# An encoder layer in split float32 matmuls: tiles that begin at multiples of 256 bytes

## The chip, the cores and the metric

The kernel runs on one core of a Trainium2 chip. The metric is the device time of one execution in microseconds (us); lower is better. TensorE is called PE below, VectorE DVE, ScalarE ACT and GpSimd POOL.

## What is computed

One layer of a bidirectional encoder over 512 tokens of width 1024, in float32:

```python
x = x + 0.5 * swiglu(rmsnorm(x), w1, w3, w2)          # first FFN, width 2816
h = rmsnorm(x)
proj = h @ w_in                                       # attention A: q,k,v; attention B: q,k,v; gates
o_a = three groups of dilated window attention, 8 heads of 64, weighted by their softmax sums
o_b = grouped attention, 8 heads of 128, 2 key/value heads, per-head norm and rotary
x = x + (sigmoid(g_a) * (o_a @ P_a) + sigmoid(g_b) * (o_b @ P_b)) @ w_out
x = x + 0.5 * swiglu(rmsnorm(x), w1, w3, w2)          # second FFN
out = rmsnorm(x)
```

## The kernel before, in words

**Split matmuls.** A float32 operand is kept as two tiles of type float32r, a high part (names in H) and the rest (names in L), and one product is three matmuls into the same bank: H by H, H by L and L by H (`mm3`, lines 232 to 234). In each, one 128x128 block is the stationary operand, loaded first, and the other operand streams through with 256 or 512 columns, the moving operand. Nearly all PE time is such matmuls.

- 512 columns, 3000 matmuls: the plain projections (moving hH, hL: 768), the token projections (`token`, moving the weights wh, wl, stationary hH, hL: 576, of which 192 take every fourth column of hH as stationary), the products with w2 (`blocks`, moving gg: 984), the branch and output products (moving oH, qH, mH: 480) and those of attention B (moving kH, kL, vH, vL: 192).
- 256 columns, 4176 matmuls: the first products of both FFNs and ten blocks of the q, k projection are done by a seven-product scheme (`strassen`) on halves of the tokens. One step is 24 matmuls (two column blocks, four row blocks, three parts), its moving operand either a half of hH, hL or a tile of sums TH, TL (in the q, k projection TQ). There are 63 steps in the first FFN, 35 in the q, k projection and 70 in the second FFN, 4032 matmuls; the last 144 are the halves of the last product with w2 (moving gg).

**The order of the work.** PE's order is that of the code. The weights come by DMA into rings (wr, wa, wt), are split by ACT and DVE into the ring of wh, wl tiles, and PE takes them from there. Every fourth of these pairs, in the stages that have the room, lies in a second ring.

**Where tiles lie.** Within a partition, tiles are laid one behind the other, each rounded up to 32 bytes. One stack grows from the low end (constants, small tiles, rings, working tiles), one from the high end (hH, hL, below them rel_bias and TH, TL). So the start of a large tile follows from the small tiles that were laid before it. By the addresses in the built program, these are the starts of the tiles that split matmuls read, in bytes past a multiple of 256:

```
tiles                                    before   after
hH, hL                                      224       0
TH, TL, first FFN                           128       0
TH, TL, second FFN                          224       0
TQ                                           32       0
gg, kH, kL, vH, vL, PTH, PTL                 32       0
oH, oL, qH, qL, mH, mL                       32       0
wh, wl, first ring                          160       0
wh, wl, second ring                          32       0
```

The 32 of gg, for example, comes from the constants (they end at 160 past a multiple) and the 16-byte tiles ms, ss and rs, four of each with 32 bytes to each (384 together). hH is at 224 since the usable memory ends 32 bytes below a multiple of 256. The identity that the transposes read begins at 64, before and after.

Of the kernel before, what the change touches and what calls it, by code (L numbers as in the profile page):

```python
# [11 lines left out]
F32 = mybir.dt.float32  # L12
# [19 lines left out]
LAG = 1  # L32
LAST = 2
WARM = 4
T = 512
D = 1024
NK = 8
# [16 lines left out]
def tile_at(li):  # L54
    if li < 4:
        return 256 * li, (256 if li < 3 else 128), (0 if li < 3 else 64)
    return GP + 256 * (li - 4), 256, 256
# [8 lines left out]
def f32(t):  # L66
    return t.bitcast(F32)


class Layer:  # L70
    def __init__(self, ctx, tc, a):
        self.tc, self.nc, self.a = tc, tc.nc, a
        ctx.enter_context(tc.manual_schedule(engines={mybir.EngineType.PE}))
        pool = lambda n, **k: ctx.enter_context(tc.tile_pool(name=n, **k))
        self.dram = pool("dram", bufs=1, space=DRAM)
        self.cst = pool("cst", bufs=1)
        self.wb = pool("wb", bufs=1)
        self.tmp = pool("tmp", bufs=4)
        self.psm = pool("psm", bufs=4, space=PSUM)
        self.psa = pool("psa", bufs=4, space=PSUM)  # L80
        nc = self.nc
        c = self.cst
        self.x = [c.tile([128, T], F32, name=f"x{d}") for d in range(NK)]
        self.par = c.tile([128, 48], F32, name="par")
        nc.scalar.dma_start(self.par, a["par"])
        self.ident = c.tile([128, 128], F32, name="ident")
        self.ones = c.tile([128, 1], F32, name="ones")
        nc.vector.memset(self.ones, 1.0)
        self.mhalf = c.tile([128, 4], F32, name="mhalf")
        nc.vector.memset(self.mhalf, -0.5)  # L90
        nc.scalar.activation(self.ones, self.ones, AF.Copy)
        self.r = c.tile([128, 8], F32, name="r")
        self.R = c.tile([128, T], F32, name="R")
        nc.gpsimd.memset(self.R, 0.0)
        self.acc = c.tile([128, T], F32, name="acc")
        self.open_h()
        self.gate_d = self.dram.tile([16, 128, T], F32, name="gate_d")
        self.qk_d = self.dram.tile([2 * NSQ, 128, T], F32, name="qk_d")
        self.items = ([("v", 0), ("v", 1), ("sw", 0), ("v", 2)] + [("g", j) for j in range(2)]
                      + [("qk", f) for f in range(NSQ, 12)] + [("g", j) for j in range(2, 9)]  # L100
                      + [("b", g) for g in range(3)] + [("g", j) for j in range(9, 16)])
        span = {"v": ("wav", 4), "qk": ("waq", 2), "g": ("wg", 1), "b": ("wb", 4)}
        self.order = self.ffn_order("a")
        for kind, n in self.items:
            if kind == "sw":
                self.order += [("swq", at) for at in self.slots(range(0, NSQ, 2))]
                continue
            name, m = span[kind]
            self.order += [(name, m * n + i) for i in range(m)]
        self.order += [("wab", i) for i in range(12)] + [("wo", i) for i in range(8)]  # L110
        self.order += self.ffn_order("b")
        self.raws, self.tiles, self.used, self.wx, self.TQ = {}, [], 0, None, None
        self.cap = len(self.order)
        self.rings = {k: [] for k in BUFS}
        self.index = {it[:2]: n for n, it in enumerate(self.order)}
        self.kind = [self.home(it) for it in self.order]
        self.todo = sorted((n for n, t in enumerate(self.kind) if t != "ws"), key=self.turn_of)
# [22 lines left out]
    def open_h(self):  # L140
        self.hctx = ExitStack()
        hp = self.hctx.enter_context(self.tc.tile_pool(name="hp", bufs=1, side="right", reuse_waits="tile"))
        self.hH = [hp.tile([128, T], F32R, name=f"hH{d}") for d in range(NK)]
        self.hL = [hp.tile([128, T], F32R, name=f"hL{d}") for d in range(NK)]
# [236 lines left out]
    def rpow(self, dst, src, inv):  # L381
        nc = self.nc
        n = dst.shape[-1]
        ms = self.tmp.tile([128, 4], F32, tag="ms", name="ms")[:, :n]
        nc.vector.tensor_scalar(ms, src, inv, EPS, op0=ALU.mult, op1=ALU.add)
        nc.gpsimd.tensor_tensor(dst, ms, self.mhalf[:, :n], op=ALU.pow)

# [194 lines left out]

    def bias_open(self, bp):
        self.bp = bp
        self.rel = bp.tile([32, 24], F32, name="rel_bias")
        self.nc.sync.dma_start(self.rel, self.a["rel_bias"])
        self.zd = self.dram.tile([8, 128, NV], F32, name="zd")
        self.vd = self.dram.tile([8, NV], F32, name="vd")
# [163 lines left out]
    def scores_a(self, hp, res):  # L752
        nc, ap, qk = self.nc, self.ap, self.qk[hp]
# [11 lines left out]
        for pair in range(4):  # L765
            banks = [self.aux("S") for _ in range(2)]
            heads = []
            for h in range(2):
                hs, ps, mv = slice(64 * h, 64 * h + 64), banks[h], []
                for u in range(2):  # L770
                    li = 2 * pair + u
                    n, o = tile_at(li)[1], 256 * u
# [6 lines left out]
                    else:  # L779
                        c = slice(128 * (li - 4), 128 * (li - 4) + 128)  # L780
# [5 lines left out]
            for h in range(2):  # L786
                for u in range(2):
                    li = 2 * pair + u
                    off, n, w0 = tile_at(li)
# [4 lines left out]
            for h in range(2):  # L794
                for li in (2 * pair, 2 * pair + 1):
                    off, n, _ = tile_at(li)
# [24 lines left out]
        nc.vector.tensor_mul(L, E, SO[:, :, :, 2:4])  # L821
        nc.vector.tensor_add(MN, L[:, 0], L[:, 1])
        nc.vector.reciprocal(MN, MN)
        F = ap.tile([128, 8, 2], F32, tag="F", name="F", bufs=2)
        nc.vector.tensor_mul(F, E[:, 0], MN)
        res += [P, F]

    def values_a(self, hp, P, F):
        nc, ap, V = self.nc, self.ap, self.V
# [8 lines left out]
        def scale(stage):  # L838
            for h in range(2):
                for li in (2 * stage, 2 * stage + 1):  # L840
                    off, n, _ = tile_at(li)
                    sl = P[h][:, off:off + n]
                    nc.vector.tensor_scalar(sl, sl, F[:, li, h:h + 1], None, op0=ALU.mult)

# [109 lines left out]
    def attn_b(self, pp):  # L954
        nc = self.nc
        qH, qL, kH, kL, vH, vL = self.qH, self.qL, self.kH, self.kL, self.vH, self.vL
        P, po, pend = {}, {}, []

        def score(h, i):
            ps = self.aux("Sb")  # L960
            s = slice(128 * i, 128 * i + 128)
            self.mm3(ps, qH[:, h, s], qL[:, h, s], kH[:, h // 4, :], kL[:, h // 4, :], True, True)
            nm = pp.tile([128, 1], F32, tag="nm", name="nm", bufs=4)
            nc.vector.tensor_reduce(nm, ps, axis=mybir.AxisListType.X, op=ALU.max, negate=True)
            p = pp.tile([128, T], F32, tag="P", name="Pb", bufs=8 + LAG)
            lq = pp.tile([128, 1], F32, tag="lq", name="lq", bufs=4)
            nc.scalar.activation(p, ps, AF.Exp, bias=nm, scale=1.0, accum_out=lq)
            nc.vector.reciprocal(lq, lq)
            nc.vector.tensor_scalar(p, p, lq, None, op0=ALU.mult)
            P[h, i] = p  # L970

        def flip(h, k):
            pt = self.aux("Tb")
            for j in range(4):
                nc.tensor.transpose(pt[:, 128 * j:128 * j + 128], P[h, j][:, 128 * k:128 * k + 128], self.ident)  # L975
            H, L = self.split(pp, pt, [128, T], "PTH", "PTL")
            fs = slice(128 * (h // 4), 128 * (h // 4) + 128)
            pend.append((h, k, vH[:, k, fs], vL[:, k, fs], H, L, k == 0, k == 3))

        def value():  # L980
            h, k, *args = pend.pop(0)
            if k == 0:
                po[h] = self.bank()
            self.mm3(po[h], *args)
            if k == 3:
                nc.scalar.copy(qH[:, h, :], po[h])
                nc.vector.tensor_sub(qL[:, h, :], po[h], f32(qH)[:, h, :])

        for s in range(37 + LAG):
            if s < 32:  # L990
                score(s // 4, s % 4)
            t = s - 4 - LAG
            if 0 <= t < 32:
                flip(t // 4, t % 4)
            if pend and t > 0:
                value()
            yield GAP_B
        assert not pend
# [95 lines left out]
    def layer(self, out):  # L1094
# [4 lines left out]
        warm = self.aux("warm")  # L1099
        for _ in range(WARM):  # L1100
            nc.tensor.matmul(warm[:, :256], self.R[:, :128], self.R[:, :256], start=True, stop=True)
# [123 lines left out]
```

## Time and profile before

| | |
|---|---|
| median of three runs | 1282.46 us (1282.14 to 1282.67) |
| profiled execution, own time | 1282.78 us |
| its span, first to last instruction | 1281.0 us |
| granted clock of PE over the span | 0.998 of full speed |
| PE busy | 1266.8 us, 99% of the span |
| DVE, ACT, POOL busy | 887.8, 586.5, 118.9 us |

A matmul counts as busy from its start to its modelled end, and matmuls overlap, so the 99% says that PE always had one in flight, not that it was at its peak. What a matmul costs is read from the distance between the starts of two that follow each other, or from the length of a stretch and the number of matmuls in it.

### The profile page before, as it was taken

What the parts mean: (1) busy time and instruction counts of PE and PEld (TensorE: products, weight loads), DVE (VectorE), ACT (ScalarE), POOL (GpSimd) and SP (SyncE); (2) the same over time, 40 slices, a digit from 0 to 9 for tenths busy, and PEclk for the clock granted to TensorE, in tenths of its full rate; (3) what the DMA queues carried; (4) which work ended last, traced back from release to release, by engine and by line L of the source; (5) the groups of instructions that cost most, each with busy time, mean ns of one, the idle gap of its engine ahead of it and who ended that gap; (6) DMA issues with size and microseconds to landing.
All of it is one profiled execution on the core that took longest, in us unless ns stands there. A gap on an engine that the chain in (4) does not pass through costs nothing.

```text
span 1281.0 us, 19956 instructions
## 1 busy us (share of the span) xinstructions
PE 1266.8 (99%) x8002; PEld 1122.1 (88%) x8002; DVE 887.8 (69%) x1339; ACT 586.5 (46%) x867; POOL 118.9 (9%) x124
## 2 busy tenths in 40 slices
PE   9999999999999999999999999999999999999997
PEld 7897999899889999877888878888889989988996
DVE  7784688467783885667557898655577747874775
ACT  8551355145463442635334465543465415532553
POOL 1111101000210212100001100000301000100001
PEclk9999999999999999999999999999999999999999
DMA  8865766241484846632232210345737636743222
GB/s 298 227 187 167 182 190 189 89 109 55 144 218 142 218 131 208 189 116 85 92 111 83 99 66 25 108 163 165 237 89 181 191 90 176 196 148 104 62 83 67
DMA packets 85549, 181.91 MB, mean 142 GB/s; under 512 B 12480, under 2 KB 19024, under 8 KB 85456
## 3 DMA queue, kind: packets, MB, share of 16 engines
q1 hardware_dynamic: 67904, 140.74, 32.6%
q0 software_dynamic: 16832, 39.34, 15.2%
q8 instruction: 63, 1.03, 0.3%
q10 hardware_dynamic: 720, 0.55, 0.1%
q14 instruction: 30, 0.25, 0.1%
HBM read 168.98 MB, written 15.29 MB: 144 GB/s over the span
## 4 chain that ended last, share of the span: by engine, by line
PE 93%; DVE 3%; issue 1%; DMA 1%; ACT 1%; POOL 0%; SPq 0%; POOLq 0%; DVEq 0%
PE mm L232 24%; PE mm L234 24%; PE mm L233 24%; PE Y L232 3%; PE Y L234 3%; PE Y L233 3%; PE X L232 2%; PE X L234 2%; PE X L233 2%; PE S L785 1%; PE mm L836 1%; PE Tb L975 1%; PE T L854 1%; PE Sb L233 0%; PE Sb L234 0%
## 5 line engine op out<-in xcount | busy, mean ns | idle before, releaser
L217 ACT CAST wh<-wr 128x1024 fp32r<-128x1024 f32 x142 | 148.8, 1049 | 224.8 <-PE mm L233 142.0
L218 DVE TENSOR_TENSOR wl<-wr,wh 128x1024 fp32r<-128x1024 f32 x142 | 173.3, 1221 | 56.9 <-ACT wh L217 56.2
L232 PE MATMUL mm<-hH,wh 128*128 128x256 f32 (+1 forms) x600 | 200.5, 334 | 0.4 <-ACT hH L368 0.3
L234 PE MATMUL mm<-hH,wl 128*128 128x256 f32 (+1 forms) x600 | 196.3, 327 | 1.0 <-DVE wl L218 1.0
L233 PE MATMUL mm<-hL,wh 128*128 128x256 f32 (+1 forms) x600 | 196.1, 327 | 0.3 <-DVE hL L369 0.3
L232 PE MATMUL mm<-gg,wh 128*128 128x512 f32 (+1 forms) x376 | 143.1, 380 | 0.0
L234 PE MATMUL mm<-gg,wl 128*128 128x512 f32 (+1 forms) x376 | 142.6, 379 | 0.0
L233 PE MATMUL mm<-gg,wh 128*128 128x512 f32 (+1 forms) x376 | 142.5, 379 | 0.0
L232 PEld LDWEIGHTS mm<-hH,wh 128*128 128x128 f32 x600 | 112.9, 188 | 14.8 <-issue 3.2
L234 PEld LDWEIGHTS mm<-hH,wl 128*128 128x128 f32 x600 | 112.7, 188 | 12.4 <-DVE wl L218 1.4
L233 PEld LDWEIGHTS mm<-hL,wh 128*128 128x128 f32 x600 | 112.8, 188 | 10.1 <-DVE hL L369 0.8
L217 ACT CAST wh<-wa 128x1024 fp32r<-128x1024 f32 x48 | 50.4, 1050 | 102.5 <-PE mm L233 49.6
L500 DVE TENSOR_TENSOR u<-mm,R 128x512 f32<-128x512 f32 (+1 forms) x52 | 33.8, 649 | 85.0 <-PE mm L234 84.7
L218 DVE TENSOR_TENSOR wl<-wt,wh 128x1024 fp32r<-128x1024 f32 x48 | 58.7, 1223 | 38.1 <-ACT wh L217 37.6
L234 PE MATMUL mm<-TH,wl 128*128 128x256 f32 x304 | 84.7, 279 | 0.0
L232 PE MATMUL mm<-TH,wh 128*128 128x256 f32 x304 | 84.6, 278 | 0.0
L233 PE MATMUL mm<-TL,wh 128*128 128x256 f32 x304 | 84.6, 278 | 0.0
L232 PEld LDWEIGHTS mm<-gg,wh 128*128 128x128 f32 x376 | 70.8, 188 | 15.3 <-PE mm L234 0.9
L234 PEld LDWEIGHTS mm<-gg,wl 128*128 128x128 f32 x376 | 70.8, 188 | 14.1
L233 PEld LDWEIGHTS mm<-gg,wh 128*128 128x128 f32 x376 | 70.9, 188 | 13.8
L217 ACT CAST wh<-ws 128x1024 fp32r<-128x1024 f32 x48 | 50.4, 1051 | 71.0 <-PE mm L233 52.3
L218 DVE TENSOR_TENSOR wl<-wa,wh 128x1024 fp32r<-128x1024 f32 x48 | 58.6, 1221 | 31.2 <-ACT wh L217 31.0
(233 smaller groups left out, 3171.3 us busy)
## 6 DMA issues: line engine op xcount, KB each, us to landing
wr<-in_w2a SPq DMA_DIRECT2D x22, 512.0 KB, 3.3
wr<-in_w2b SPq DMA_DIRECT2D x22, 512.0 KB, 3.5
wt<-in_w13b SPq DMA_DIRECT2D x20, 512.0 KB, 4.1
wa<-in_w13b SPq DMA_DIRECT2D x20, 512.0 KB, 3.5
wt<-in_w13b POOLq DMA_DIRECT2D x20, 512.0 KB, 6.1
wt<-in_w13a SPq DMA_DIRECT2D x18, 512.0 KB, 3.5
wt<-in_w13a POOLq DMA_DIRECT2D x18, 512.0 KB, 6.2
wa<-in_w13a SPq DMA_DIRECT2D x18, 512.0 KB, 3.4
```

The lines of the kernel that those rows point to most:

```text
L217: self.nc.scalar.copy(H, raw)
L218: self.nc.vector.tensor_sub(L, raw, f32(H))
L232: mm(out, lH, rH, start=start, stop=False, skip_group_check=more)
L233: mm(out, lH, rL, start=False, stop=False, skip_group_check=more)
L234: mm(out, lL, rH, start=False, stop=stop, skip_group_check=more)
L500: nc.vector.tensor_mul(u, ps, R)
L785: nc.tensor.matmul(*args, start=True, stop=True)
L836: nc.tensor.matmul(oc, v, p, start=st, stop=sp)
L854: nc.tensor.transpose(ps[:, 128 * b:128 * b + 128], P[h][:, c0 + 128 * b:c0 + 128 * b + 128], self.ident)
L975: nc.tensor.transpose(pt[:, 128 * j:128 * j + 128], P[h, j][:, 128 * k:128 * k + 128], self.ident)
```

## The change

Two filler tiles, and small tiles of round sizes. `edge`, 224 bytes, is the first tile of the stack at the high end; `even`, 96 bytes, stands among the constants; nothing reads or writes either. ms, nm and lq are made 64 bytes, rel_bias 256 and F 128, of which slices of the former sizes are used. In the built program every tile that a split matmul reads begins at a multiple of 256 bytes (the table above). The built program of the change has the same instructions on every engine, in the same order, with the same waits: what differs is addresses, and the row lengths of the five enlarged tiles.

```diff
+EDGE = 224
...
+        self.edge = ctx.enter_context(tc.tile_pool(name="edge", bufs=1, side="right")).tile([128, EDGE // 4], F32, name="edge")
...
         self.r = c.tile([128, 8], F32, name="r")
+        c.tile([128, 24], F32, name="even")
...
-        ms = self.tmp.tile([128, 4], F32, tag="ms", name="ms")[:, :n]
+        ms = self.tmp.tile([128, 16], F32, tag="ms", name="ms")[:, :n]
...
-        self.rel = bp.tile([32, 24], F32, name="rel_bias")
+        self.rel = bp.tile([32, 64], F32, name="rel_bias")[:, :24]
...
-        F = ap.tile([128, 8, 2], F32, tag="F", name="F", bufs=2)
+        F = ap.tile([128, 16, 2], F32, tag="F", name="F", bufs=2)[:, :8]
...
-            nm = pp.tile([128, 1], F32, tag="nm", name="nm", bufs=4)
+            nm = pp.tile([128, 16], F32, tag="nm", name="nm", bufs=4)[:, :1]
...
-            lq = pp.tile([128, 1], F32, tag="lq", name="lq", bufs=4)
+            lq = pp.tile([128, 16], F32, tag="lq", name="lq", bufs=4)[:, :1]
```

## Rows read from the trace of the kernel before

**Rows 1.** The page: the chain that ended last, shares of the span.

```profile
PE 93%; DVE 3%; issue 1%; DMA 1%; ACT 1%; POOL 0%; SPq 0%; POOLq 0%; DVEq 0%
```

**Rows 2.** PE's longest waits: us in total, times, longest.

```profile
PE mm L836 <- DVE PT L856: 1.6, 1, 1.6
PE warm L1101 <- POOL R L94: 1.3, 1, 1.3
PE rb L401 <- POOL r L386: 1.0, 1, 1.0
```

**Rows 3.** Windows, 256-column stages: length, PE busy (matmuls), clock, DMA share, GB/s.

```profile
53.44:92.46 39.02, 39.02 (x336) 1.00 0.68 176
139.36:218.00 78.64, 78.64 (x672) 1.00 0.72 188
262.54:321.56 59.02, 59.02 (x504) 1.00 0.29 84
402.09:501.35 99.26, 99.26 (x840) 1.00 0.60 176
954.99:1012.74 57.75, 57.75 (x504) 1.00 0.71 185
1057.28:1133.53 76.25, 76.25 (x672) 1.00 0.72 189
1178.07:1235.28 57.21, 57.21 (x504) 1.00 0.29 86
1252.04:1261.90 9.86, 9.86 (x84) 1.00 0.00 0
```

**Rows 4.** Windows, 256 columns: one or two steps of 24 matmuls, start to start.

```profile
142.19:145.06 2.87, 2.87 (x26) 1.00 0.56 191
181.83:187.51 5.68, 5.68 (x50) 1.00 0.51 164
407.77:410.62 2.85, 2.85 (x26) 1.00 0.72 210
1257.74:1260.60 2.86, 2.86 (x26) 1.00 0.00 0
```

**Rows 5.** Windows, 512 columns; up to three matmuls counted only overlap an edge.

```profile
29.31:53.20 23.89, 23.89 (x107) 1.00 0.97 288
817.90:936.90 119.00, 119.00 (x515) 1.00 0.59 183
649.28:675.60 26.32, 26.32 (x115) 1.00 0.28 91
378.50:401.60 23.10, 23.10 (x98) 1.00 0.40 113
1144.80:1150.24 5.44, 5.44 (x25) 1.00 0.26 90
```

**Rows 6.** Timeline of four transposes: start, us to the last end; and the next start.

```profile
780.49 0.60 PE L975 MATMUL Tb<-ident,Pb 128*128 128x128 f32 x4
780.85 0.48 PE L232 MATMUL mm<-PTH,vH 128*128 128x512 f32 x1
```

**Rows 7.** Groups by shape: busy us, mean ns of one.

```profile
L975 PE MATMUL Tb<-ident,Pb 128*128 128x128 f32 x128 | 19.4, 273 | 0.2 <-DVE Pb L969 0.2
```

**Rows 8.** Windows, all engines, second FFN: busy of PE, weight loads, DVE, ACT, POOL.

```profile
1057.28:1133.53 76.25, 76.25 (x672) 76.25 (x671) 62.23 (x62) 41.53 (x47) 8.43 (x7) 1.00 0.72 189
```

## The prediction

> **What bounds the kernel now.** I read the chain of waits first: 93% of the span is PE, and DVE, DMA and ACT share the rest [rows 1]. Then PE's waits: the longest is 1.6 us and there are a handful [rows 2]. So PE is not waiting for tiles; the time is the number of matmuls times their pace. The pace is therefore what I looked at next, in stretches that hold split matmuls of one width alone.
>
> For 256 columns the stages do not agree, although their matmuls have the same shape [rows 3]. In the first FFN 336, 672 and 504 matmuls take 39.02, 78.64 and 59.02 us: 116.1, 117.0 and 117.1 ns each. The q, k projection takes 118.2 (99.26 us over 840). The second FFN, which issues the same steps as the first, takes 114.6, 113.5 and 113.5. The last half products take 9.86 us over 84, 117.4, or about 119 when the two that only overlap an edge are taken off. The granted clock is 1.00 in every one of these rows, which is the 2.4 GHz level. It is not traffic either: the slow last row has a DMA share of 0.00, and in the second FFN 0.72 and 0.29 give the same 113.5 [rows 3]. What differs between the stages is where their tiles begin. In the second FFN all moving tiles begin at 224 past a multiple of 256; in the first, TH is at 128 and hH at 224; in the projection TQ is at 32 and hH at 224.
>
> Single steps say the same [rows 4]. A step with TH at 128 takes 119.6 ns a matmul (2.87 us over 24) when its weights lie in the second ring, at 32, and 118.3 (5.68 us over 48) when they lie in the first, at 160. TQ at 32 with weights at 32 takes 118.8 (2.85 over 24), and gg at 32 with weights at 32 takes 119.2 (2.86 over 24).
>
> For 512 columns [rows 5], with the edge matmuls taken off: hH at 224 with weights at 160 takes 229.7 (23.89 us over 104); tiles at 32 with weights at 160 take 232.4 (119.00 over 512); the token products 233 (26.32 over 113), and where the stationary operand takes every fourth column 238 (23.10 over 97). Moving gg at 32 with weights also at 32 takes 226.7 (5.44 over 24).
>
> **What the change does, part by part.** No instruction is added, removed or moved, and no wait changes. The fillers are never touched, and the larger small tiles are used in the same sizes, so those edits cost nothing in themselves. DVE's and ACT's instructions on tiles at new starts could take another time, but in the densest stage DVE is busy 62.23 of 76.25 us and ACT 41.53 [rows 8], so a few per cent there stay covered; were DVE 20% slower it would reach PE's 76 us. Loads land at new starts too; DMA is 1% of the chain, most of it at the start [rows 1]. I take zero for these, within 2 us either way. What is left is the pace of 7176 split matmuls. No row shows a tile at 0 past a multiple of 256, so each width is bounded by the nearest rows.
>
> *512 columns.* After the change moving and stationary tiles begin at the same place, as gg and the second ring do now, at 32 both. That row is the nearest: 227 ns. By classes: 1200 matmuls at 32 with weights at 160, (232.4 - 227) ns each, 6.5 us; 768 with hH at 224, (229.7 - 227), 2.1 us; 384 token products in contiguous columns, (233 - 227), 2.3 us; together 10.9 us. The 192 with every fourth column I leave, since what sets them apart stays (2.1 us if they go to 227 too). Bounds: nothing gained, or 10.9 + 2.1 = 13.0 us; below 227 see the third rival.
>
> *256 columns.* The stages of rows 3 that make up the 4032 add up to 467.15 us, 115.9 ns each. The lower bound is the second FFN's best, 113.5: 457.6 us, 9.5 us less, and 0.8 us less in the last 144 (119 to 113.5). The upper bound is what the same rows say of moving and stationary at the same place, 119.2: 480.6 us, 13.5 us more. The two neighbours point to opposite ends. I choose by what the second FFN has and the others lack: its moving tiles all begin at one place, while weights alternate between 160 and 32 without harm, and it has the fastest of all stages. After the change there is one place for everything. I take the mean of that FFN, (57.75 + 76.25 + 57.21) us over 1680, 113.8 ns: 458.9 us, 8.3 us less, and 0.7 for the last 144, 9.0 us in all.
>
> The sum is 10.9 + 9.0 = 20 us. The profiled execution took 1282.78 us with a span of 1281.0, and the median of the runs is 1282.46, 0.3 us from it; from the median the forecast is 1262 us.
>
> **A rule weighed.** Two 512-column matmuls with gg at 32 stand 227 or 232 ns apart, by whether their weights begin at 32 or at 160 [rows 5], so the read of the weights does reach into the moving stream. The Trainium skill, SBUF — State Buffer, SBUF: two separate sides, says that PE never waits on anyone at its memory ports; by it the pace would have nothing to do with where tiles lie, and the time would stay at 1282.5. The rows do not agree with it for two reads of PE itself.
>
> **Rivals.**
>
> *Tiles that begin at the same place get in each other's way (slower).* For it: the two 256-column rows with both at 32 are among the slowest (118.8 and 119.2), and TH at 128, the only moving tile that begins at a multiple of 128, is slow too (118.3 and 119.6) [rows 4]: being rounder is no help there. With 256 columns a weight load must fit into the time of one matmul; with 512 it has twice that, so a collision could cost the one and not the other. Against it: rows with one and the same collision should be slow at 512 too, and are the fastest. Price: 13.5 us lost at 256 columns, 10.9 won at 512, 1285 us; if the 512 columns do not gain, 1296. It decides from a mean of 115.9 + 10.9 us / 4032 = 118.6 ns on.
>
> *Nothing changes.* All tiles begin at a multiple of 32 now, and if the unit that matters is no larger, the differences between stages come from something else that the change leaves, such as distances between tiles. 1282.5 us, give or take 3. The Trainium skill, SBUF — State Buffer, Specifications (TRN2), gives lines of 16 bytes, and by that unit alone no line would be saved; no run here shows the unit.
>
> *The floor falls.* The fastest rows, 113.5 and 227, are in one ratio to the columns, 0.443 ns each, and all their moving tiles begin off a multiple of 64. Four transposes take 0.60 us with a last one of 273 ns, so they start (600 - 273) / 3 = 109 ns apart [rows 6, 7]. If a start at a round place lets 256 columns pass in 109 and 512 in 218, the sum is 4032 x 6.9 + 144 x 10 = 29 us and 1200 x 14.4 + 768 x 11.7 + 384 x 15 + 456 x 9 = 36 us, 65 us, 1217 us; half of it is 1250. Against it: TH at 128 does begin at a multiple of 64 and shows none of this. The Trainium skill, TensorE: Matmul & The Clock Gate, Back-to-back issue gap, gives columns / 2.4 + 2.5 ns, 109 and 216; by it the time would be an estimate of 1211.
>
> **How the numbers follow.** Forecast, a gain of 10 to 30 us: 0.38. Floor falls, a gain beyond that: 0.14. Nothing, or gains and losses that cancel within some 10 us: 0.22. Collisions, a loss of more than that or of nearly that: 0.26. About 0.2%, 2.6 us, is what a measurement of this kernel can tell from no change. Of the cancelling cases a little under half lies within it, and the rest falls on both sides: faster 0.56, same 0.11, slower 0.33. The range for 8 in 10 leaves out the deep half of the fallen floor and the worst collisions (no gain at 512 columns and 119.6 at 256): 1228 to 1297. The likeliest case alone spans 1252 to 1273.
>
> **What would show it.** In the profile after, the stretches of rows 3 and 5 hold the same matmuls, so their lengths compare one to one. Right: the first FFN's and the projection's steps as quick as the second FFN's, near 113.5 to 114, and the products with w2 and the branches near 227. The floor has fallen if any 512-column stretch is below 224. The collision rival shows as 119 and more in the second FFN, which is at 113.5 now. Wrong in its base would be a PE that begins to wait, for instance on DVE's wl tiles, or a pace that still differs between stages although all tiles begin alike.

## The result, and the profile after

The change makes the kernel slower: 1287.8 us, median of six runs (1287.2 to 1288.61), against 1282.51 for the kernel before in six runs beside it (1282.14 to 1282.83). The ratio is 1.0041, 95% interval 1.0029 to 1.0054. The forecast was 1262 us and faster. The profiled execution's span is 1286.2 us, before 1281.0. Line numbers after are three higher than before.

The chain of waits, by engine, and then PE's longest waits (us in total, times, longest), answer to [rows 1, 2]:

```profile
PE 90%; DVE 4%; issue 1%; DMA 1%; ACT 1%; POOL 1%; SPq 1%; POOLq 0%; DVEq 0%
```

```profile
PE warm L1104 <- POOL R L97: 1.3, 1, 1.3
PE rb L404 <- POOL r L389: 1.0, 1, 1.0
PE mm L237 <- DVE wl L221: 1.0, 1, 1.0
```

PE still waits for nothing that matters. The 256-column stages in windows, in the order of [rows 3]: window, length and PE busy, matmuls, clock, DMA share, GB/s. Each window runs from the start of a stage's first matmul to that of its last, so a length is divided by one less than the stage's matmuls, in all windows of this part.

```profile
52.94:93.13 40.19, 40.19 (x336) 1.00 0.67 172
139.28:219.79 80.51, 80.51 (x672) 1.00 0.72 183
263.46:323.81 60.35, 60.35 (x504) 1.00 0.29 83
402.92:503.59 100.67, 100.67 (x840) 1.00 0.60 173
952.07:1012.42 60.35, 60.35 (x504) 1.00 0.70 182
1056.08:1136.60 80.52, 80.52 (x672) 1.00 0.68 180
1180.26:1240.62 60.36, 60.36 (x504) 1.00 0.28 83
1257.08:1267.04 9.96, 9.96 (x84) 1.00 0.00 0
```

All stages now have one pace: 80.51 us over 671 distances, 100.67 over 839 and 60.36 over 503 are 120.0 ns each. Before, the same division of [rows 3] gives 116.5, 117.2, 117.3 and 118.3 ns, and 114.8, 113.6 and 113.7 in the second FFN. The eight windows add up to 492.91 us, against 477.07 before when cut in the same way (the lengths of [rows 3] add up to 477.01): 15.8 us lost.

The 512-column windows lie in the same stages as [rows 5], cut to starts, so that each holds one or two matmuls fewer:

```profile
29.34:52.49 23.15, 23.15 (x103) 1.00 0.99 294
818.17:933.87 115.70, 115.70 (x511) 1.00 0.61 188
650.75:675.93 25.18, 25.18 (x112) 1.00 0.29 95
379.68:402.22 22.54, 22.54 (x97) 1.00 0.43 116
1147.85:1153.06 5.21, 5.21 (x24) 1.00 0.25 85
```

The contiguous ones are all at 226.5 to 227.0 ns (115.70 us over 510 is 226.9), where they were 229.7, 232.4 and 233; the last, gg with its weights in the second ring, was at 226.7 already. Those with every fourth column as stationary come to 234.8 from 238. The span grew by 5.2 us, so everything outside the 256-column stages gained 15.8 - 5.2 = 10.6 us.

Three groups by shape (busy us, mean ns of one) of weight loads: hH and gg have both widths, TH has 256 columns alone.

```profile
L235 PEld LDWEIGHTS mm<-hH,wh 128*128 128x128 f32 x600 | 114.3, 191 | 14.1 <-issue 3.2 <-ACT wh L220 0.4 <-ACT wh L1114 0.4
L235 PEld LDWEIGHTS mm<-gg,wh 128*128 128x128 f32 x376 | 70.8, 188 | 14.1 <-PE mm L237 0.9 <-issue 0.6
L235 PEld LDWEIGHTS mm<-TH,wh 128*128 128x128 f32 x304 | 58.4, 192 | 0.0
```

The loads for TH take 192 ns, those for hH, more than half of them beside 256-column matmuls, 191, and those for gg, mostly beside 512-column ones, 188.

### The profile page after: what moved, and what is told of

Its sections match the earlier page's. It is cut to its first block, busy times and chain, and to the rows that moved or that the text cites. A ratio compares the mean times of both kernels' runs of the same rounds, so it can differ in the third digit from the quotient of the medians.

```text
span 1286.2 us, 19956 instructions
## 1 busy us (share of the span) xinstructions
PE 1272.6 (99%) x8002; PEld 1136.9 (88%) x8002; DVE 888.8 (69%) x1339; ACT 586.3 (46%) x867; POOL 119.5 (9%) x124
## 4 chain that ended last, share of the span: by engine, by line
PE 90%; DVE 4%; issue 1%; DMA 1%; ACT 1%; POOL 1%; SPq 1%; POOLq 0%; DVEq 0%
PE mm L235 23%; PE mm L237 23%; PE mm L236 23%; PE Y L237 4%; PE Y L236 4%; PE Y L235 4%; PE X L237 2%; PE X L236 2%; PE X L235 2%; PE mm L839 1%; PE Tb L978 1%; PE S L788 1%; DVE wl L221 1%; PE T L857 1%; DMA d<-SO 1%
## 5 line engine op out<-in xcount | busy, mean ns | idle before, releaser
L235 PE MATMUL mm<-hH,wh 128*128 128x256 f32 (+1 forms) x600 | 202.0, 337 | 0.0
L235 PE MATMUL mm<-gg,wh 128*128 128x512 f32 (+1 forms) x376 | 141.8, 377 | 0.0
L235 PEld LDWEIGHTS mm<-hH,wh 128*128 128x128 f32 x600 | 114.3, 191 | 14.1 <-issue 3.2
L235 PE MATMUL mm<-TH,wh 128*128 128x256 f32 x304 | 86.0, 283 | 0.0
L235 PEld LDWEIGHTS mm<-gg,wh 128*128 128x128 f32 x376 | 70.8, 188 | 14.1 <-PE mm L237 0.9
```

The source lines that it names most:

```text
L235: mm(out, lH, rH, start=start, stop=False, skip_group_check=more)
```

## Experiments

Below, "difference" is the start of the stationary operand minus that of the moving one, in bytes modulo 256. Times are medians, with the ratio to the kernel before on the same chip and its 95% interval; the latter had medians of 1282.17 to 1283.21 us.

**All starts at 32 instead of 0** (against the changed kernel):

```diff
-EDGE = 224
+EDGE = 192
...
-        c.tile([128, 24], F32, name="even")
+        c.tile([128, 32], F32, name="even")
```

> Every split operand, moving and stationary, begins 32 bytes past a multiple of 256 and no longer on one; all differences of starts stay zero. Theory 1 (only the difference of the stationary operand's start from the moving operand's, modulo 256 bytes, sets the pace): nothing changes against the changed kernel, 256-column matmuls 120.0 ns, 512-column ones 226.8 ns, 1287.8 us within 1.5 us. Theory 2 (being on a multiple of 256 bytes is itself what sets the pace): the 256-column matmuls leave 120.0 ns by 1 ns or more, 1283 us or less, or the 512-column ones go back to 231 ns, 1297 us.

Measured: 1288.67 us, ratio 1.0051 (1.0034 to 1.0068). Windows of the projection and of the second FFN's longest stage:

```profile
403.25:503.92 100.67, 100.67 (x842) 1.00 0.62 173
1056.78:1137.30 80.52, 80.52 (x674) 1.00 0.68 180
```

Nothing moves, to the hundredth of a us. A multiple of 256 is not what counts; theory 2 falls.

**256-column moving tiles at 64, then at 192**, weights at 0 (changed kernel with one number altered):

```diff
-EDGE = 224
+EDGE = 160
```

> The changed kernel with a right-hand filler of 160 bytes a row: the hidden halves and token halves that 256-column matmuls read (hH, hL, TH, TL) begin at 64, the weights at 0, so the difference (stationary minus moving) is 192 for 3552 of the 4032 matmuls of the full 256-column stages; the 480 of the query tokens (TQ) stay at 0 against 0. Theory 1: the 3552 take one of the two settled paces that the kernel before shows at this difference, 113.3 ns (3552 x 6.7 = 23.7 us less, about 1266 us with 2 us lost on the 512-column matmuls of hH) or 117.7 ns (8 us less, about 1282 us); the 480 stay at 120.0 ns. Theory 2 (a start on a multiple of 64 bytes is what costs): 120.0 ns everywhere, 1288 us.

```diff
-EDGE = 224
+EDGE = 32
```

> As the run with starts at 64, but hH, hL, TH and TL at 192 (filler of 32 bytes a row), so the difference is 64, at which the kernel before went into the 113.3 ns pace. Theory 1: 3552 matmuls at 113.3 ns, the 480 of the query tokens at 120.0 ns, 512-column matmuls of hH 226.8 to 229.6 ns: 1287.8 - 23.7 + 2 = about 1266 us. Theory 2: 120.0 ns everywhere, 1288 us.

Measured: 1283.65 us, 1.0005 (0.9995 to 1.0014), and 1280.73 us, 0.9985 (0.9976 to 0.9995). Windows of the run with 64, in the first FFN, the projection and the second FFN (of each FFN the longest stage):

```profile
138.90:217.93 79.03, 79.03 (x672) 1.00 0.72 186
400.78:500.73 99.95, 99.95 (x840) 1.00 0.61 174
1054.40:1133.43 79.03, 79.03 (x672) 1.00 0.71 183
```

And with 192, the first FFN's first two stages and the projection:

```profile
55.15:93.12 37.97, 37.97 (x337) 1.00 0.71 175
139.25:218.28 79.03, 79.03 (x673) 1.00 0.73 186
400.82:499.09 98.27, 98.27 (x841) 1.00 0.62 177
```

The weight loads for TH in the run with 64:

```profile
L235 PEld LDWEIGHTS mm<-TH,wh 128*128 128x128 f32 x304 | 57.1, 188 | 0.0
```

Moving the start alone takes the pace off 120.0 ns. At a difference of 192 it is 117.8 ns (79.03 over 671). At 64 there are two settled paces for one and the same work: the first stage runs at 113.3 (37.97 over 335), later ones at 117.8. That is why the second run missed its 1266 us. In the projection, where its hH steps follow TQ steps at a difference of 0, the window is 1.68 us shorter than in the run with 64: the quicker pace seems to be entered from a difference of 0. That became theory 3, with its rival theory 4; both are put in the expectation of the run with the larger bias tile.

**The right-hand filler alone** (against the kernel before):

```diff
+EDGE = 224
...
+        self.edge = ctx.enter_context(tc.tile_pool(name="edge", bufs=1, side="right")).tile([128, EDGE // 4], F32, name="edge")
```

> The kernel before with the right-hand filler alone: hH and hL move from 224 to 0, TH and TL from 128/224 to 160/0, the weights stay at 160/32 and alternate. The differences of hH become 160 and 32 instead of 192 and 64. Theory 1: hH goes from about 115 ns to the 118 to 120 ns that the kernel before shows at 160 and 32, 2184 x 4 = 9 us more, nothing won at 512 columns: 1288 to 1294 us. Theory 2 (round starts of one operand decide): about half of the change's effect on both kinds of matmul, 1282 to 1286 us.

Measured: 1298.43 us, 1.0122 (1.0107 to 1.0137), worse than the whole change. Windows of the first and of the second FFN:

```profile
140.69:220.87 80.18, 80.18 (x673) 1.00 0.72 184
1065.53:1145.72 80.19, 80.19 (x673) 1.00 0.69 181
```

119.5 ns in both, with differences of 0, 32, 128 and 160 in the first FFN and of 32 and 160 in the second, and nothing won at 512 columns. The direction fits theory 1. The size was set too low: it priced hH alone, while TH and TL of the second FFN leave 64 and 192 as well.

**One size alone, and three mixtures.** First the bias tile (against the kernel before):

```diff
-        self.rel = bp.tile([32, 24], F32, name="rel_bias")
+        self.rel = bp.tile([32, 64], F32, name="rel_bias")[:, :24]
```

> The kernel before with one size changed: the bias tile has 64 columns instead of 24, so TH and TL of the first feed-forward begin at 224 as in the second, with hH, instead of at 128; weights still alternate between 160 and 32. Theory 3 (the 113.3 ns pace is entered at a difference of 64 that follows another difference, and kept at 64 and 192): the three 256-column stages of the first feed-forward go from 117.1 ns to the second one's 113.9 ns, 1512 x 3.2 = 4.8 us less, about 1277.5 us; the query and key projection keeps 118.3 ns. Theory 4 (which of the two paces a stage gets is settled by how it begins, and the tiles in between don't alter it): 117 ns as before, 1282.5 us.

Measured: 1278.75 us, 0.9962 (0.9948 to 0.9976): one small tile's size makes the kernel faster. Windows of the longest stage of the first FFN, the projection and the longest stage of the second FFN:

```profile
139.08:215.66 76.58, 76.58 (x672) 1.00 0.73 191
398.29:497.56 99.27, 99.27 (x840) 1.00 0.61 175
1053.20:1129.46 76.26, 76.26 (x672) 1.00 0.72 189
```

The first FFN's stage goes from 78.64 us [rows 3] to 76.58, 114.1 ns; the projection and the second FFN stay. The observation behind the forecast was right: one place for the moving tiles, with weights that take turns 128 bytes apart, is quick. But its differences are 64 and 192, not 0.

Next, hH and hL at 192 with TH and TL at 0 (the changed kernel with EDGE = 32, and behind TL):

```diff
+            tp.tile([128, 48], F32, name="drop")
```

> The run with hidden halves at 192 again, but the token halves TH and TL at 0, as the query tokens were: 2184 matmuls of hH and hL at a difference of 64, 1848 of the token halves at 0. Theory 3: every group of hH that follows a token group takes 113.3 ns, in all stages as in the query and key projection of the run before, and the token groups take 120.0 ns: 2184 x 6.7 = 14.6 us less than the changed kernel, 3 to 4 us lost on the 512-column matmuls of hH, about 1277 us. Theory 4: hH at 117.7 ns except in the first stage and the projection, about 1284 us.

Measured: 1277.32 us, 0.9953 (0.9939 to 0.9967). Windows of the first 24 matmuls of the first FFN's second stage (hH), then of 48 of hH and 48 of TH and TL further on in it:

```profile
138.98:141.69 2.71, 2.71 (x25) 1.00 0.93 135
150.30:155.63 5.33, 5.33 (x50) 1.00 0.83 181
161.42:167.06 5.64, 5.64 (x50) 1.00 0.50 161
```

The first step of hH takes 117.8 ns (over 23); behind steps of TH, hH takes 113.4 and TH 120.0 (over 47), within one stage, at the same clock. That is theory 3, in a stage that stayed at 117.8 ns when TH was at 192 too. Theory 4 falls in its second half: the tiles in between do alter the pace.

Then hH at 192 with TH and TQ at 64, and the reverse (the changed kernel with EDGE = 32 and 160; the figures of the first):

```diff
             self.TL = tp.tile([128, 3, 4, 256], F32R, name="TL")
+            tp.tile([128, 32], F32, name="drop")
...
+            tp.tile([128, 16], F32, name="lift")
             self.TQ = [tp.tile([128, 4, 4, 256], F32R, name=f"TQ{c}") for c in "HL"]
+            tp.tile([128, 48], F32, name="fill")
```

> Hidden halves at 192 (difference 64), token halves TH, TL and the query tokens TQ at 64 (difference 192), all else at 0: the two differences take turns, as with the second feed-forward of the kernel before. Theory 3: within the first groups of each 256-column stage the pace goes to 113.3 ns and stays: 4032 x 6.7 = 27 us less than the changed kernel, 3 to 4 us lost on the 512-column matmuls of hH, about 1264 us, faster than both kernels. Theory 4: 117.7 ns in the feed-forwards' later stages, about 1279 us.

> The same with the places exchanged: hidden halves at 64 (difference 192), token halves and query tokens at 192 (difference 64). Theory 3: 113.3 ns from the first token group of each 256-column stage on, about 1264 us. Theory 4: 117.7 ns, about 1280 us. The stages begin with hH, here at the difference at which the run with all at 192 never left 117.7 ns.

Measured: 1280.29 us, 0.9977 (0.9967 to 0.9986), and 1280.77 us, 0.9981 (0.9972 to 0.999). Windows of the first of the two, 48 of hH and 48 of TH, TL in the first stage, then the whole second stage, then the projection: 48 of hH, 48 of TQ, and the whole:

```profile
65.47:70.80 5.33, 5.33 (x50) 1.00 0.80 170
76.58:82.12 5.54, 5.54 (x50) 1.00 0.49 155
139.14:218.17 79.03, 79.03 (x673) 1.00 0.72 185
409.18:414.51 5.33, 5.33 (x50) 1.00 1.05 272
414.62:420.16 5.54, 5.54 (x50) 1.00 0.42 77
400.79:498.08 97.29, 97.29 (x841) 1.00 0.62 179
```

Theory 3 as it was put falls here: a change of difference between 64 and 192 does not bring the quick pace when it is the moving tile that changes (113.4 and 117.9 ns in turn in the first stage and in the projection, 117.8 throughout the second stage; in the reverse run, too, the second stage stays at 117.8), though it does when the weights change. Theory 3b took its place: the quick pace is entered from a difference of 0. It does not account for everything. The first stage, and here the projection too, run at 113.4 ns at a difference of 64 with no 256-column matmul at 0 in them, while the stages behind the products with w2, whose 512-column matmuls are at a difference of 0, stay at 117.8. So the quick projection of the run with 192 does not by itself speak for theory 3b, and how a stage begins counts as well, as the first half of theory 4 has it; what about the beginning decides is open.

**The first tiles alone at 0**: weights at 0, EDGE = 32, the fillers around TQ exchanged and "drop" of 16 columns so that TH, TL and TQ lie at 192 with hH and hL, but for the first pair, or hL0 alone, which stay at 0. The part of the first run's edit that splits hH and hL, against the changed kernel:

```diff
-        self.hH = [hp.tile([128, T], F32R, name=f"hH{d}") for d in range(NK)]
-        self.hL = [hp.tile([128, T], F32R, name=f"hL{d}") for d in range(NK)]
+        pad = lambda n: hp.tile([128, n // 4], F32, name="pad")
+        mk = lambda c, d: hp.tile([128, T], F32R, name=f"h{c}{d}")
+        self.hH, self.hL = [mk("H", 0)], [mk("L", 0)]
+        pad(192)
+        self.hH += [mk("H", d) for d in range(1, NK)]
+        self.hL += [mk("L", d) for d in range(1, NK)]
```

> Weights and all tiles of 512-column work at 0 as in the changed kernel; hH and hL at 192 but for their first tiles hH0 and hL0, which stay at 0; TH, TL and the query tokens at 192 too. 258 of the 4032 matmuls of the full 256-column stages are at a difference of 0, 3774 at 64. Theory 3b (at a difference of 64 the 113.3 ns pace is entered from a matmul at a difference of 0, not from one at 192): every stage begins with hH0, goes on with hH1 at 113.3 ns and keeps that pace through the token groups; 3774 x 6.7 = 25 us less than the changed kernel, 4 us lost on the 512-column matmuls of hH, about 1267 us, faster than all kernels so far. Theory 4 (a few matmuls at 0 don't alter it; whole groups must): 117.7 ns in the later stages, about 1281 us.

> The same with hL0 alone at 0 (86 matmuls, each between two at a difference of 64) and hH0 at 192 with the rest. Theory 3b: one matmul at a difference of 0 is enough, 3946 x 6.7 = 26 us less than the changed kernel, 4 us lost at 512 columns, about 1266 us. Theory 4: 117.7 ns in the later stages, about 1280 us.

Measured: 1266.89 us, 0.988 (0.9863 to 0.9896), and 1266.57 us, 0.9878 (0.9863 to 0.9892): both faster than both kernels by more than 1%. Windows of the run with hL0 alone: first FFN, projection, second FFN, and then the first 512-column projections and the branch and output products:

```profile
138.05:214.53 76.48, 76.48 (x672) 1.00 0.75 191
395.09:490.46 95.37, 95.37 (x840) 1.00 0.63 182
1041.72:1118.20 76.48, 76.48 (x672) 1.00 0.71 188
29.52:53.27 23.75, 23.75 (x104) 1.00 0.98 297
806.32:922.15 115.83, 115.83 (x512) 1.00 0.60 188
```

114.0, 113.7 and 114.0 ns: a few matmuls at a difference of 0 in a stage are enough, and the pace holds through the token steps behind them, in the stages behind the products with w2 as well. Of 512 columns, the products keep 227.1 ns (over 510), while hH, now at a difference of 64, gives back some (232.8 ns over 102, against 227.0 in the changed kernel). The loads' groups by shape show 188 ns, no longer 191 and 192 (L239 is L235 of the changed kernel):

```profile
L239 PEld LDWEIGHTS mm<-hH,wh 128*128 128x128 f32 x600 | 112.8, 188 | 14.9 <-issue 3.2 <-ACT wh L1121 0.4 <-ACT hH L375 0.4
L239 PEld LDWEIGHTS mm<-TH,wh 128*128 128x128 f32 x304 | 57.1, 188 | 0.0
```

**The bias tile and TQ at 224** (the kernel before with the larger bias tile, and 48 and 16 columns of filler around TQ):

```diff
+            tp.tile([128, 48], F32, name="lift")
             self.TQ = [tp.tile([128, 4, 4, 256], F32R, name=f"TQ{c}") for c in "HL"]
+            tp.tile([128, 16], F32, name="fill")
```

> The run with the bias tile of 64 columns, with the query tokens too at 224 instead of 32, so that every 256-column moving tile but gg begins at one place and the weights take turns between 160 and 32; the 512-column work as in the kernel before. Theory 3b as seen there: with one moving place and weights that change by 128 the 113.3 ns pace is entered and kept: the 840 matmuls of the query and key projection go from 118.4 ns to about 114 ns, 3.7 us less than that run, 1275 us. Against it: its stage keeps 117.7 ns, 1278 us.

Measured: 1275.16 us, 0.9944 (0.9929 to 0.9958). The window of the projection:

```profile
398.18:493.48 95.30, 95.30 (x841) 1.00 0.63 182
```

113.6 ns instead of 118.3 [rows 3]: the quick pace is entered here with no matmul of these stages at a difference of 0, by weights that change.

**The other part of the change alone** (the changed kernel without the right-hand filler):

```diff
-EDGE = 224
...
-        self.edge = ctx.enter_context(tc.tile_pool(name="edge", bufs=1, side="right")).tile([128, EDGE // 4], F32, name="edge")
```

> The other part of the change alone: the left-hand filler and the small tiles of round sizes, without the right-hand filler. Weights, gg and the query tokens at 0, hH, hL, TH and TL at 224: differences 32 for 3552 of the 4032 matmuls, 0 for the 480 of the query tokens. By the theory of differences: 118.2 ns (measured at 32 in the kernel before and with the right-hand filler alone) and 120.0 ns, 10 us lost against the kernel before; the 512-column matmuls of gg and the branches at 0 win 10 us: about 1283 us. If the two parts simply add up (the whole change +5 us, the right-hand filler alone +15 us): 1272 us.

Measured: 1286.39 us, 1.0031 (1.0018 to 1.0043). Windows of the first FFN and of the projection:

```profile
139.46:218.86 79.40, 79.40 (x673) 1.00 0.71 186
401.84:501.77 99.93, 99.93 (x841) 1.00 0.61 174
```

118.3 ns at a difference of 32, as expected; the whole missed by 3 us. All 256-column windows of this run add up to 486.88 us, 9.8 more than before, while its span is 3.1 us longer, so everything else, the 512 columns above all, won 6.7 us and not 10. The parts do not add up: +15.3 and +4.0 us alone, +5.3 together, since each moves only one side of the difference.

## Why the prediction was wrong

*What bounds the kernel* was right: PE waits for nothing in either kernel, and in every run the time follows the pace of split matmuls, at a clock of 1.00 in every window shown. The edits that were costed at nothing cost nothing that shows: no wait of PE above 1.3 us in the changed kernel.

*512 columns* was right. The choice of 227 ns, from the one row with both operands at the same place, is what was measured (226.5 to 227.0), and 10.9 us forecast stand against 10.6 gained outside the 256-column stages. A little of that comes from the 192 matmuls that the forecast had left alone (234.8 from 238). Some readings of the rows were off without bearing on the sum: the row at 232 ns [rows 5] holds the branch and output products, not gg; the paces read from [rows 3] divide by the matmuls and not by the distances between them, and are 0.1 to 0.4 ns low; and 9.86 us over 84 less two matmuls would be 120.2 ns, where the 119 that was used is the length over 83 distances.

*256 columns* is the step that failed: "I take the mean of that FFN, 113.8 ns", for "after the change there is one place for everything". The gain of 9.0 us turned into a loss of 15.8. The second FFN's pace came from differences of 64 and 192 between weights and moving tiles, which the change takes away, and not from a common place of the moving tiles as such: the larger bias tile gave the first FFN these differences, and its longest stage went to 114.1 ns. At a difference of 0 the pace is 120.0 ns, at 0 and at 32 alike (the run with all starts at 32). The rows for this stood in the prediction as the upper bound: 118.8 and 119.2 ns with both at 32 [rows 4]. They were the nearest rows, the only ones with the difference that the change makes general, and for 512 columns the nearest row was taken. At the upper bound for 256 columns the sum would have been 13.5 - 10.9, 1285 us, the time that the rival gave.

*The slower rival* is what happened, in direction and in how it divides: the same start costs 256 columns and helps 512. That the tiles get in each other's way, the reason it gave, no run shows. Its price was 13.5 us at 256 columns where 15.8 were lost, as a stage that is at this difference throughout has 120.0 ns and not 119.2.

*The other rivals.* "Nothing changes" fell with the first of these runs. "The floor falls" did too: no 512-column window read here is below 226.5 ns, and no 256-column one below 113.3. The Trainium skill, TensorE: Matmul & The Clock Gate, Back-to-back issue gap, gives the formula that the prediction weighed there for the gap of a single matmul by itself, which the prediction left out.

*The rule weighed.* The Trainium skill, SBUF — State Buffer, SBUF: two separate sides, says that PE never waits on anyone at its memory ports. Where that is taken to mean, as the prediction took it, that the pace has nothing to do with where tiles lie, the runs do not agree: the changed kernel and the one with EDGE = 32 differ in the length of a filler that nothing reads, their matmuls come in the same order, and the pace goes from 120.0 to 113.3 or 117.8 ns. Whether the time is lost at the memory ports no run shows.

What the runs show is the dependence on the difference, and that the pace at 64 and 192 depends on what ran before. That it is the read of the next weights which collides with the moving stream is argued, not shown. The longer loads at a difference of 0 (192 ns for TH at 120.0) and one pace at DMA shares from 0.00 to 0.72 fit it; but the loads for TH take 188 ns in the run at 117.8 and in the one at 114.0 alike, so the length of a load does not tell these two paces apart. Open too is why weights that change by 128 bytes bring the quick pace and a moving tile that changes by 128 does not, and what about the beginning of a stage decides between the two.

## What to carry to other kernels

Where matmuls with a load each follow one another without a wait, look at the pace stage by stage, and set it against where both operands begin, as a difference and not tile by tile: round starts for all were worth a loss of 0.4% here, and other starts a gain of 1.2%. A nearest row counts for more than a fast stage whose reason is only guessed: what the change makes general must be what the fast row has. And an odd size of a small tile can move every large tile behind it, so a change of any size in such a kernel can be a change of pace too: one bias tile was worth 0.4% here.

## What the runs showed of the hardware

- Split matmuls of 256 columns, with all weights at one place, have settled paces that depend on the difference of starts: 120.0 ns at 0 (the changed kernel), 118.3 at 32 (without the right-hand filler), 117.8 at 192 (EDGE = 160), 113.3 or 117.8 at 64 (EDGE = 32). With 512 columns it is the other way round: 227 ns at 0 (the changed kernel), 232.8 at 64 (hL0 alone at 0).
- At 64 the quicker pace is a state: one and the same work ran at 113.3 or 117.8 ns by what ran ahead of it. It was entered behind 256-column matmuls at a difference of 0, by weights that change by 128 bytes under one moving place, or at the beginning of some stages, for a reason that is open. Where the weights take turns it is kept at 192 as well (113.6 ns over 76.25 us of the second FFN before [rows 3], where 64 and 192 take turns, and over the projection with TQ at 224); where the moving tiles do, those at 192 take 117.9 ns between others at 113.4.
- At a difference of 0 it makes no difference whether the tiles begin at 0 or at 32: 100.67 us over the projection in both.
- A weight load beside 256-column matmuls took 192 ns at a difference of 0 and 188 ns at 192 and at 64 (TH in the changed kernel, in the run with EDGE = 160 and with hL0 alone at 0), at paces of 120.0, 117.8 and 114.0 ns.
